# The down projection of a squared-ReLU MLP by seven products of tile sums in chunks 0 to 6

## The chip, the cores and the metric

The kernel runs on one core of one Trainium2 chip. The metric is the device time of one execution in microseconds (us), from runs without a profile; the profile is that of one more execution. TensorE (PE) multiplies, VectorE (DVE) and ScalarE (ACT) work element by element, GpSimd (POOL) and SyncE (SP) issue transfers here, and SBUF and PSUM are the memories on the core: TensorE writes only to PSUM, in banks of 512 floats in each of 128 partitions.

## The reference

One layer of a streaming encoder for 384 tokens: 256 of a new stream and 8 x 16 of running streams. A mixer (a pooling branch and a state-space branch) is followed by the MLP, and the MLP's second product is what the change touches:

```python
D_MODEL = 2048
D_FF = 4 * D_MODEL

x = x + rmsnorm(m, p['g_mix_post'])
hdn = jnp.square(jax.nn.relu(rmsnorm(x, p['g_mlp_pre']) @ p['w_up'])) @ p['w_down']
x = x + rmsnorm(hdn, p['g_mlp_post'])
```

All inputs and outputs are float32.

## The kernel before

**Float32 by three products.** Every operand of a large product is split into a high part, rounded to the format that TensorE multiplies at full speed (`F32R`), and a low part, the rest. A product is then high x high + high x low + low x high, three matmuls into the same bank. `wfetch` (L61) loads a weight tile of 128 x 1024 floats (512 KB) into the ring `w` on SyncE's queue. `wsplit` (L66) makes the high part `wh` on ScalarE (L70) and the low part `wl` on VectorE (L71). The rings `w`, `wh` and `wl` have three tiles each (`wpool`, L39), shared by the up and the down projection.

**Chunks.** The MLP runs in eight chunks (`c8`, L1408) of 1024 hidden channels. The *up stage* of a chunk makes eight hidden tiles (`f8`, L1410): `proj` (L136) multiplies two weight tiles of `w_up` with the 16 tiles of the normed input, 48 matmuls of 384 columns into one bank of `psm` (two banks, L40). VectorE applies the relu and the norm's factor, ScalarE squares, and the result `ht` (channels in the partitions, 384 tokens in the columns) is split into `hh` and `hl`.

The *down stage* multiplies these eight tiles with the chunk's rows of `w_down`, for each of four blocks of 512 output columns (`nb`, L1424): `moving` (L145) takes four weight tiles (`kp`), each with two rows of 128 channels (`k2`), and for each row and each of three blocks `b` of 128 tokens issues the three matmuls of 512 columns (L154 to L156). Here the hidden tile is the stationary operand and the weight moves through. So one `kp` is 18 matmuls and a down stage 4 x 4 x 18 = 288. The three sums of a column block stand in three banks of `pss` (six banks, L41). `done` (L1431) adds each to the accumulator `hacc` in SBUF on VectorE (L1439); in chunk 0 ScalarE copies it there (L1434).

In the last chunk `done` goes on: squares for the norm (L1443), the scale `gpo` (L1445), and behind the last column block the norm's factor, the residual with `x1` (L1455) and the stores of `y`. The very last block's third sum is seeded: ScalarE copies the accumulator into the bank first (L1429) and the matmuls add to it.

**Memory.** `x1` (the residual stream, 3 x 128 x 2048 floats) lies in SBUF from the mixer to the end, as do `gpo`, loaded on GpSimd's queue (L1403) and scaled on ScalarE (L1404), and the split normed input (`x1h`, `x1l`). `mp` and the phase `phf` ahead of the MLP use the right side of SBUF.

**Order.** A tile framework fixes the order of each engine's instructions and all semaphores when the program is made. It does not have to keep the order of the code; where the code wants an order, it says so with `behind`, which the down stage of chunks 0 to 6 does not.

Of the kernel before, what the change touches and what calls it, by code (L numbers as in the profile page):

```python
# [14 lines left out]
P = 128  # L15
T = 384
TP = 256
NB = 8
TS_ = 16
DM = 2048  # L20
# [13 lines left out]
def build(ctx, tc, io):  # L34
    nc = tc.nc
    v, s, te, gp, sy = nc.vector, nc.scalar, nc.tensor, nc.gpsimd, nc.sync

    consts = ctx.enter_context(tc.tile_pool(name="consts", bufs=1))
    wpool = ctx.enter_context(tc.tile_pool(name="wpool", bufs=3))  # L39
    psm = ctx.enter_context(tc.tile_pool(name="psm", bufs=2, space=PSUM))  # L40
    pss = ctx.enter_context(tc.tile_pool(name="pss", bufs=6, space=PSUM))  # L41
    dram = ctx.enter_context(tc.tile_pool(name="dram", bufs=1, space=DRAM))
# [10 lines left out]
    def sstile(name):  # L53
        return pss.tile([P, 512], F32, tag="ss", name=name)
# [51 lines left out]
    bank = [mmtile]  # L106
# [232 lines left out]
    for k in range(4, KD, 2):  # L339
        xsplit(k)  # L340
        xsplit(k + 1)
        hl = esplit(k)
# [780 lines left out]
    r2 = res.tile([P, T], F32, name="r2")  # L1123

    root = [None, None]

# [17 lines left out]
    for b in range(3):  # L1144
        sy.dma_start(x1[:, b, :], io["x_tok"][b])
    NE = 4
    pg0 = ctx.enter_context(tc.tile_pool(name="pg0", bufs=1, reuse_waits="tile"))
    xs2 = []

    def xtiles(pool, n):  # L1150
# [5 lines left out]
    with tc.tile_pool(name="phf", bufs=1, side="right", reuse_waits="tile") as pf, tc.tile_pool(  # L1156
# [119 lines left out]
                {(2, 3): first_turns} if nb == 3 else None,  # L1276
            )
        phk.close()
        pga = ctx.enter_context(tc.tile_pool(name="pga", bufs=1, reuse_waits="tile"))
# [94 lines left out]
        chain[0] = False  # L1374
        for b, i in ((1, 2), (1, 3), (2, 0), (2, 1), (2, 2), (2, 3)):
            square(b, i)
        u20 = chained(io["w_up"][2, 0], "up2_0")
        dgh = pf.tile([P, 3, P], F32R, name="dgh2")
        dgl = pf.tile([P, 3, P], F32R, name="dgl2")
# [13 lines left out]
            last[0] = te.matmul(pairs(bc), onesr, woven(dgl.rearrange("p b t -> p (b t)")), start=False, stop=True)  # L1393
        prod((2,), range(12, KD))
        s.copy(halves(r2), even_odd(bc))
    mpool.close()

    with tc.tile_pool(name="phg", bufs=1, reuse_waits="tile") as pg, tc.tile_pool(
        name="phg2", bufs=2, reuse_waits="tile"
    ) as pg2:  # L1400
        hacc = pg.tile([P, 3, DM], F32, name="hacc")
        gpo = pg.tile([P, DM], F32, name="gpo2")
        gp.dma_start(gpo, io["g_mlp_post"].partition_broadcast(P))  # L1403
        s.activation(gpo, gpo, AF.Copy, scale=-0.5)  # L1404
        st3 = pg.tile([P, 3, 4], F32, name="st3")
        pg.tile([P, 112], F32, name="pad_e")
        NC = 8
        for c8 in range(NC):  # L1408
            hh = []
            for f8 in range(8):  # L1410
                f = c8 * 8 + f8
                ps = ups[f] if f < 3 else proj([io["w_up"][f, 0], io["w_up"][f, 1]], xs2, f"up{f}")
                t = pg2.tile([P, T], F32, tag="t", name=f"ht{f}")
                for c, w in ((slice(0, TP), slice(0, P)), (slice(TP, T), slice(P, 192))):
                    v.scalar_tensor_tensor(
                        out=halves(t[:, c]), in0=even_odd(ps)[:, :, w], scalar=0.0, in1=halves(r2[:, c]), op0=ALU.max, op1=ALU.mult
                    )
                s.activation(t, t, AF.Square)
                h = pg2.tile([P, T], F32R, tag=f"hh{f8}", name=f"hh{f}", bufs=1)
                l = pg2.tile([P, T], F32R, tag=f"hl{f8}", name=f"hl{f}", bufs=1)  # L1420
                s.activation(h, t, AF.Copy)
                v.tensor_tensor(l, t, h.bitcast(F32), ALU.subtract)
                hh.append((h, l))
            for nb in range(4):  # L1424
                o = [sstile(f"wd{c8}_{nb}_{b}") for b in range(3)]
                end = c8 == NC - 1 and nb == 3
                held = 2 if end else None
                if end:
                    s.copy(o[held], hacc[:, held, blk(nb)])  # L1429

                def done(b):  # L1431
                    dst = hacc[:, b, blk(nb)]
                    if c8 == 0:
                        s.copy(dst, o[b])  # L1434
                        return
                    if b == held:
                        dst = o[b]
                    else:
                        v.tensor_tensor(dst, o[b], dst, ALU.add)  # L1439
                    if c8 < NC - 1:  # L1440
                        return
                    q = pg2.tile([P, 512], F32, tag="q3", name=f"q3_{nb}_{b}")
                    s.activation(q, dst, AF.Square, accum_out=st3[:, b, nb : nb + 1])  # L1443
                    if nb < 3:
                        v.tensor_tensor(dst, dst, gpo[:, blk(nb)], ALU.mult)  # L1445
                        return
                    if b == 0:
                        pg.tile([P, 128], F32, name="pad_z")
                    z3 = pg.tile([P, 512], F32, name=f"z3_{b}")
                    v.tensor_tensor(z3, dst, gpo[:, blk(nb)], ALU.mult)  # L1450
                    y = postnorm(pg2, st3, b, "n3", doubled=True)
                    for i in range(4):
                        z = z3 if i == 3 else hacc[:, b, blk(i)]
                        for n, c in enumerate((slice(0, 256), slice(256, 512)) if b + i == 5 else (slice(0, 512),)):
                            v.scalar_tensor_tensor(  # L1455
                                out=z[:, c], in0=z[:, c], scalar=y, in1=x1[:, b, blk(i)][:, c], op0=ALU.mult, op1=ALU.add
                            )
                            (s if n else sy).dma_start(io["y"][b][:, blk(i)][:, c], z[:, c])

                moving(  # L1460
                    o,
                    [(io["w_down"][c8, nb, kp], f"wd{c8}_{nb}_{kp}") for kp in range(4)],
                    hh,
                    4 if end else 0,
                    done,
                    pg,
                    2 if end else 0,
                    held=held,
                )


def _consts(np):
# [121 lines left out]
```

## Time and profile before

| what | us |
|---|---|
| median of 3 runs (2633.67 to 2634.31) | 2634.19 |
| span of the profiled execution (first to last instruction) | 2631.4 |
| up stage of chunk 2 (384 matmuls) | 62.40 |
| down stage of chunk 2 (288 matmuls) | 62.16 |

For the profiled execution the profile gives only the span, not the time around it; median and span are 2.8 us apart. In the profile's rows L is a line of the kernel, the part behind the engine is the operation with its output and inputs by the program's names, then shapes and a count, busy time and mean ns of one, and the idle time of the engine just before them with what ended it. PE is the matmul stream, PEld its weight loads, SPq and POOLq the transfers issued by these engines with their size and the us from issue to landing. In a table of windows each engine has its busy us and its instructions, then follow the granted TensorE clock, the mean busy share of the DMA engines and GB/s.

### The profile page before, as it was taken

Reading aid. Unit: us, or ns where it says so; the run is one execution under the profiler, and the core shown is the slowest. Engines: PE = TensorE matmul, PEld = TensorE weight load, DVE = VectorE, ACT = ScalarE, POOL = GpSimd, SP = SyncE. Lnnn points to the kernel's source line nnn. Section 1 sums busy time; section 2 is a strip of 40 time slices with the busy share of each in tenths; the row PEclk is TensorE's granted clock in tenths of the full one; section 3 lists DMA queues with packets and bytes.
Section 4 is the critical chain, followed back from the end, with each engine's and each line's share of the span. In section 5 each row is a group of like instructions: output and inputs, shape, how many; then the busy total and the mean of one; then the engine's idle time right before and its main releaser. Section 6 shows DMA issues by size and latency. Waiting matters only on the chain.

```text
span 2631.4 us, 40780 instructions
## 1 busy us (share of the span) xinstructions
PE 2621.3 (100%) x16189; PEld 2523.4 (96%) x16189; DVE 1573.0 (60%) x2286; ACT 1159.7 (44%) x1789; POOL 368.6 (14%) x545
## 2 busy tenths in 40 slices
PE   9999999999999999999999999999999999999998
PEld 9999999999999999999999989999999999989897
DVE  6685335799999999967444436434444444444446
ACT  6443324657565756555333336433333333333233
POOL 0000003245444444411000000000000000000000
PEclk9999999999999999999999999999999999999999
DMA  7445446667676767757545544444444444444443
GB/s 276 150 133 156 148 147 223 201 210 238 224 239 211 235 228 238 233 188 260 165 160 160 195 149 133 144 136 136 134 134 135 136 136 136 136 136 136 135 135 131
DMA packets 134256, 456.33 MB, mean 173 GB/s; under 512 B 20545, under 2 KB 27521, under 8 KB 129073
## 3 DMA queue, kind: packets, MB, share of 16 engines
q1 hardware_dynamic: 103552, 361.44, 43.0%
q0 software_dynamic: 23456, 77.47, 8.5%
q10 hardware_dynamic: 7056, 14.81, 1.8%
q8 instruction: 127, 2.08, 0.3%
q14 instruction: 65, 0.52, 0.1%
HBM read 409.27 MB, written 44.37 MB: 172 GB/s over the span
## 4 chain that ended last, share of the span: by engine, by line
PE 99%; DMA 0%; DVE 0%; ACT 0%; SPq 0%; issue 0%; DVEq 0%
PE pj_up L101 6%; PE pj_up L103 6%; PE pj_up L102 6%; PE wd L156 6%; PE wd L155 6%; PE wd L154 6%; PE pj_x L101 5%; PE pj_x L102 5%; PE pj_x L103 5%; PE pj_sp L102 3%; PE pj_z L103 3%; PE pj_z L102 3%; PE pj_z L101 3%; PE pj_sp L103 3%; PE pj_sp L101 3%; PE pj_gb L101 2%
## 5 line engine op out<-in xcount | busy, mean ns | idle before, releaser
L101 PE MATMUL pj_up<-x1h,wh_up 128*128 128x384 f32 (+1 forms) x1024 | 333.7, 326 | 0.0
L103 PE MATMUL pj_up<-x1h,wl_up 128*128 128x384 f32 (+1 forms) x1024 | 333.4, 326 | 0.0
L102 PE MATMUL pj_up<-x1l,wh_up 128*128 128x384 f32 (+1 forms) x1024 | 333.4, 326 | 0.0
L71 DVE TENSOR_TENSOR wl_wd<-w_wd,wh_wd 128x1024 fp32r<-128x1024 f32 x126 | 154.4, 1225 | 240.3 <-ACT wh_wd L70 240.3
L154 PE MATMUL wd<-wh_wd,hh 128*128 128x512 f32 x756 | 286.5, 379 | 0.0
L155 PE MATMUL wd<-wl_wd,hh 128*128 128x512 f32 x756 | 286.5, 379 | 0.0
L156 PE MATMUL wd<-wh_wd,hl 128*128 128x512 f32 x756 | 286.5, 379 | 0.0
L70 ACT ACTIVATE wh_wd<-w_wd 128x1024 fp32r<-128x1024 f32 x126 | 133.1, 1057 | 321.5 <-PE wd L156 261.0
L70 ACT ACTIVATE wh_up<-w_up 128x1024 fp32r<-128x1024 f32 x126 | 133.1, 1057 | 291.9 <-PE pj_up L102 231.7
L71 DVE TENSOR_TENSOR wl_up<-w_up,wh_up 128x1024 fp32r<-128x1024 f32 x126 | 154.4, 1225 | 178.1 <-ACT wh_up L70 178.0
L101 PE MATMUL pj_x<-xgh,wh_x 128*128 128x384 f32 x768 | 251.9, 328 | 0.0
L102 PE MATMUL pj_x<-xgl,wh_x 128*128 128x384 f32 x768 | 250.4, 326 | 0.0
L103 PE MATMUL pj_x<-xgh,wl_x 128*128 128x384 f32 x768 | 250.4, 326 | 0.0
L102 PEld LDWEIGHTS pj_up<-x1l,wh_up 128*128 128x128 f32 x1024 | 193.6, 189 | 0.2
L101 PEld LDWEIGHTS pj_up<-x1h,wh_up 128*128 128x128 f32 x1024 | 193.6, 189 | 0.2
L103 PEld LDWEIGHTS pj_up<-x1h,wl_up 128*128 128x128 f32 x1024 | 193.6, 189 | 0.0
L101 PE MATMUL pj_z<-xgh,wh_z 128*128 128x384 f32 x512 | 166.9, 326 | 0.0
L102 PE MATMUL pj_z<-xgl,wh_z 128*128 128x384 f32 x512 | 166.9, 326 | 0.0
L103 PE MATMUL pj_z<-xgh,wl_z 128*128 128x384 f32 x512 | 166.9, 326 | 0.0
L101 PE MATMUL pj_sp<-abh,wh_sp 128*128 128x384 f32 x512 | 166.9, 326 | 0.0
L102 PE MATMUL pj_sp<-abl,wh_sp 128*128 128x384 f32 x512 | 166.9, 326 | 0.0
L103 PE MATMUL pj_sp<-abh,wl_sp 128*128 128x384 f32 x512 | 166.9, 326 | 0.0
(351 smaller groups left out, 6373.6 us busy)
## 6 DMA issues: line engine op xcount, KB each, us to landing
w_up<-w_up SPq DMA_DIRECT2D x128, 512.0 KB, 3.5
w_wd<-w_down SPq DMA_DIRECT2D x128, 512.0 KB, 3.5
w_x<-w_in SPq DMA_DIRECT2D x96, 512.0 KB, 3.9
w_z<-w_in SPq DMA_DIRECT2D x64, 512.0 KB, 4.4
w_sp<-w_ssd SPq DMA_DIRECT2D x64, 512.0 KB, 3.5
w_ga<-w_ga SPq DMA_DIRECT2D x32, 512.0 KB, 3.6
w_pp<-w_pp SPq DMA_DIRECT2D x32, 512.0 KB, 3.4
hs<-ssm POOLq DMA_DIRECT2D x16, 1024.0 KB, 6.3
```

The lines of the kernel that those rows point to most:

```text
L70: cut[0] = s.activation(h, w, AF.Copy)
L71: cut[1] = v.tensor_tensor(l, w, h.bitcast(F32), ALU.subtract)
L101: te.matmul(out, wh, xh, start=first, stop=False, **how)
L102: te.matmul(out, wh, xl, start=False, stop=False, **how)
L103: return te.matmul(out, wl, xh, start=False, stop=last, **how)
L154: te.matmul(out, mh, vh, start=k == 0 and b != held, stop=False, skip_group_check=b == held)
L155: te.matmul(out, mh, vl, start=False, stop=False, skip_group_check=b == held)
L156: last[0] = te.matmul(out, ml, vh, start=False, stop=k == nk - 1, skip_group_check=b == held)
```

## The change

In chunks 0 to 6 the down stage of two column blocks (a *pair*, `np_`) is computed from sums of tiles. A hidden tile has its ten slots of 128 columns: for channel rows `i` = 1 and 2 (the parity of `kp`), slots 0 to 2 are the three token blocks of row 1 and slots 3 to 5 those of row 2. Slots 6 to 9 and slot 1 are then made on VectorE: s6 = s1 - s4, s7 = s0 - s6, s8 = s3 - s7, s9 = s5 - s2, and s1 becomes s1 - s0. All ten are split in one go (`FH`, `FL`, one pair of tiles for each half `g` of the chunk's channels).

With b11, b12, b21, b22 the weight tiles of channel row i and column block j, the weight sums are U = b11 + b12, V = b12 + b22, W = U + b22 and X = b21 + W. Each of the seven tiles that are used (b11, U, V, b22, W, b21, X) is split and multiplied: for token blocks 0 and 1 seven products m0 to m6 (s0 b11, s3 b21, s8 b22, s4 X, s6 U, s7 W, s1 V), for token block 2 the two sums m7 = s2 b11 + s5 b21 and m8 = s9 b22 + s2 V. These are 11 uses of a weight tile, of 6 matmuls each, for each of two `g`: 132 matmuls for a pair, 264 for a chunk.

U, W and X are added on VectorE, in place. V is made by a transfer on GpSimd's queue that reads b22 once more from HBM and adds it to b12 in SBUF (`accum_op`), behind U's sum. The raw weights lie in nine tiles: two of three in a new ring `wd` of six, the third in `w`.

Each of the nine results has its own accumulator in `acc`. From chunk 1 on m0 to m6 are seeded: ScalarE copies the accumulator into the bank, the matmuls add to it, and ScalarE copies it back; m7 and m8 are added on VectorE as before. m0 to m6 use the six banks of `pss`, m7 and m8 the two of `psm`. In the last chunk's up stage seven sums on VectorE (`converted`) turn the accumulators of the products into those of the output blocks, and the last down stage runs as before, on slots 0 to 5.

For room `x1` is moved to the right side, stored to HBM on GpSimd's queue before the MLP and, with `gpo`, loaded back when the last up product is done and the normed input's room is free. The MLP's tiles now lie on the right side.

```diff
-    x1 = res.tile([P, 3, DM], F32, name="x1")
+    x1 = xp.tile([P, 3, DM], F32, name="x1")
+    x1_scr = [dram.tile([P, DM], F32, name=f"x1_scr{b}") for b in range(3)]
...
+        for b in range(3):
+            gp.dma_start(x1_scr[b], x1[:, b, :])
...
+        HALVES = (("b11", "U", "V"), ("b22", "W", "b21", "X"))
+        USES = {
+            "b11": ((0, 0), (7, 2)),
+            "b21": ((1, 3), (7, 5)),
+            "b22": ((2, 8), (8, 9)),
+            "X": ((3, 4),),
+            "U": ((4, 6),),
+            "W": ((5, 7),),
+            "V": ((6, 1), (8, 2)),
+        }
+        SEEDED = (0, 1, 2, 3, 4, 5, 6)
...
+        def ff_tile(f8, ps, plain):
...
+            s.activation(t, t, AF.Square)
+            if plain:
+                h, l = (a[g][:, p, q * 3 : q * 3 + 3, :].rearrange("p s t -> p (s t)") for a in (FH, FL))
+                s.activation(h, t, AF.Copy)
+                v.tensor_tensor(l, t, h.bitcast(F32), ALU.subtract)
+            elif q:
+                x = V2[p]
+                for o, a, b in ((6, 1, 4), (7, 0, 6), (8, 3, 7), (9, 5, 2), (1, 1, 0)):
+                    v.tensor_tensor(x[:, o], x[:, a], x[:, b], ALU.subtract)
+                s.activation(FH[g][:, p], x, AF.Copy)
+                v.tensor_tensor(FL[g][:, p], x, FH[g][:, p].bitcast(F32), ALU.subtract)
+
+        acc = pg.tile([P, 18, 512], F32, name="acc")
...
+        def raw(name):
+            nraw[0] += 1
+            if nraw[0] % 3 == 0:
+                return wpool.tile([P, 1024], F32, tag="w", name=f"w_{name}")
+            return pg.tile([P, 1024], F32, tag="wd", name=f"w_{name}", bufs=6)
...
+            def form(f, g):
+                k = lambda n: kept[n, g]
+                if f in ("b11", "b21", "b22"):
+                    return load(f, g, int(f[1]), int(f[2]))
+                if f == "U":
+                    kept["b12", g] = load("b12", g, 1, 2)
+                    return add(k("b11"), k("b11"), k("b12"))
+                if f == "V":
+                    gp.dma_start(k("b12"), src(2, 2, g), accum_op=ALU.add)
+                    return k("b12")
+                if f == "W":
+                    return add(k("U"), k("U"), k("b22"))
+                return add(k("b21"), k("b21"), k("W"))
+
+            def taken(m):
+                o, dst = bank[m], acc[:, np_ * 9 + m, :]
+                if c8 == 0 or m in SEEDED:
+                    s.copy(dst, o)
+                else:
+                    v.tensor_tensor(dst, o, dst, ALU.add)
+
+            for part in HALVES:
+                for g in range(2):
+                    for f in part:
+                        w = kept[f, g] = form(f, g)
+                        wh, wl = split(w, f"{f}{c8}_{np_}{g}")
+                        for m, slot in USES[f]:
+                            if m not in bank:
+                                bank[m] = (mmtile if m > 6 else sstile)(f"wd{c8}_{np_}_{m}")
+                                if c8 and m in SEEDED:
+                                    s.copy(bank[m], acc[:, np_ * 9 + m, :])
+                            held = c8 > 0 and m in SEEDED
+                            for k2 in range(2):
...
+                                te.matmul(out, mh, vh, start=begin and not held, stop=False, skip_group_check=held)
+                                te.matmul(out, mh, vl, start=False, stop=False, skip_group_check=held)
+                                te.matmul(out, ml, vh, start=False, stop=end, skip_group_check=held)
+                            if g and final[m] == f:
+                                taken(m)
...
         for c8 in range(NC):
-            hh = []
+            plain = c8 == NC - 1
+            if plain:
+                todo = converted()
             for f8 in range(8):
                 f = c8 * 8 + f8
                 ps = ups[f] if f < 3 else proj([io["w_up"][f, 0], io["w_up"][f, 1]], xs2, f"up{f}")
...
+                ff_tile(f8, ps, plain)
+                if todo:
+                    todo.pop(0)()
+            if not plain:
+                for np_ in range(2):
+                    down_pair(c8, np_)
+        upool.close()
+        pz = ctx.enter_context(tc.tile_pool(name="pz", bufs=1, reuse_waits="tile"))
+        x1 = pz.tile([P, 3, DM], F32, name="x1b")
+        gpo = pz.tile([P, DM], F32, name="gpo2")
+        gp.dma_start(gpo, io["g_mlp_post"].partition_broadcast(P))
+        for b in range(3):
+            gp.dma_start(x1[:, b, :], x1_scr[b])
+        s.activation(gpo, gpo, AF.Copy, scale=-0.5)
```

More of the change, by code (lines that the diff above doesn't have):

```diff
@@ L1146, in build @@
     NE = 4
-    pg0 = ctx.enter_context(tc.tile_pool(name="pg0", bufs=1, reuse_waits="tile"))
+    upool = ExitStack()
+    pg0 = upool.enter_context(tc.tile_pool(name="pg0", bufs=1, reuse_waits="tile"))
     xs2 = []
@@ L1412, in build @@
                 ps = ups[f] if f < 3 else proj([io["w_up"][f, 0], io["w_up"][f, 1]], xs2, f"up{f}")
[L1413 to L1469, printed above, removed]
@@ new lines, in build, with done @@
+        for nb in range(4):
+            o = [sstile(f"wd{c8}_{nb}_{b}") for b in range(3)]
+            end = nb == 3
+            held = 2 if end else None
+            if end:
+                s.copy(o[held], hacc(held, nb))
+            def done(b):
+                dst = hacc(b, nb)
+                if b == held:
+                    dst = o[b]
+                else:
+                    v.tensor_tensor(dst, o[b], dst, ALU.add)
+                q = pz.tile([P, 512], F32, tag="q3", name=f"q3_{nb}_{b}", bufs=2)
+                s.activation(q, dst, AF.Square, accum_out=st3[:, b, nb : nb + 1])
+                if nb < 3:
+                    v.tensor_tensor(dst, dst, gpo[:, blk(nb)], ALU.mult)
+                    return
+                z3 = pz.tile([P, 512], F32, name=f"z3_{b}")
+                v.tensor_tensor(z3, dst, gpo[:, blk(nb)], ALU.mult)
+                y = postnorm(pz, st3, b, "n3", doubled=True)
+                for i in range(4):
+                    z = z3 if i == 3 else hacc(b, i)
+                    for n, c in enumerate((slice(0, 256), slice(256, 512)) if b + i == 5 else (slice(0, 512),)):
+                        v.scalar_tensor_tensor(
+                            out=z[:, c], in0=z[:, c], scalar=y, in1=x1[:, b, blk(i)][:, c], op0=ALU.mult, op1=ALU.add
+                        )
+                        (s if n else sy).dma_start(io["y"][b][:, blk(i)][:, c], z[:, c])
+            moving(
+                o,
+                [(io["w_down"][c8, nb, kp], f"wd{c8}_{nb}_{kp}") for kp in range(4)],
+                hh,
+                4 if end else 0,
+                done,
+                Own,
+                2 if end else 0,
+                held=held,
+            )
```

84 lines of the change are left out of this document (75 added, 9 removed).

## The prediction

> **What bounds the kernel now.** I read the head of the page first, then the chain of work that ended last, then the stage that the change touches.
>
> ```profile
> span 2631.4 us, 40780 instructions
> PE 2621.3 (100%) x16189; PEld 2523.4 (96%) x16189; DVE 1573.0 (60%) x2286; ACT 1159.7 (44%) x1789; POOL 368.6 (14%) x545
> PEclk9999999999999999999999999999999999999999
> PE 99%; DMA 0%; DVE 0%; ACT 0%; SPq 0%; issue 0%; DVEq 0%
> ```
>
> TensorE is never idle, at full clock, and 99% of the chain is its own. So the time is the number of matmuls by the distance between them, and every wait that the change brings to TensorE is paid in full. A matmul's row lasts longer than that distance, because matmuls overlap; the distance I take from starts. These are the first matmul of chunk 2's down stage and the first of the next up stage, in the timeline of PE:
>
> ```profile
> 1938.06 0.38 PE L154 MATMUL wd<-wh_wd,hh 128*128 128x512 f32 x1
> ...
> 2000.22 0.33 PE L101 MATMUL pj_up<-x1h,wh_up 128*128 128x384 f32 x1
> ```
>
> 62.16 us for 4 x 4 x 18 = 288 matmuls is 0.2158 us each. The windows of this down stage and of the up stage behind it show what the others do meanwhile:
>
> ```profile
> 1938.06:2000.22 62.16, 62.16 (x290) 54.44 (x289) 27.75 (x30) 17.85 (x18) 0.00 (x0) 1.00 0.44 135
> 2000.22:2062.62 62.40, 62.40 (x385) 62.40 (x384) 28.12 (x39) 23.50 (x30) 0.00 (x0) 1.00 0.44 135
> ```
>
> In the down stage VectorE is busy 27.8 and ScalarE 17.9 of 62.2 us, GpSimd not at all; DMA is at 0.44.
>
> **What goes: matmuls.** A chunk now has 11 uses of a weight tile where it had 12 (seven for token blocks 0 and 1 instead of eight, four for block 2), so 264 matmuls instead of 288. 24 x 7 chunks x 0.2158 = **36.3 us** less. The last chunk stays as it was.
>
> **What comes, on VectorE and ScalarE.** The durations:
>
> ```profile
> L71 DVE TENSOR_TENSOR wl_wd<-w_wd,wh_wd 128x1024 fp32r<-128x1024 f32 x126 | 154.4, 1225 | 240.3 <-ACT wh_wd L70 240.3
> L850 DVE TENSOR_TENSOR E<-E,cbm 128x1024 f32<-128x1024 f32 x32 | 38.0, 1211 | 0.0
> L1439 DVE TENSOR_TENSOR hacc<-wd,hacc 128x512 f32<-128x512 f32 x83 | 54.9, 691 | 7.9 <-PE wd L156 7.9
> L70 ACT ACTIVATE wh_wd<-w_wd 128x1024 fp32r<-128x1024 f32 x126 | 133.1, 1057 | 321.5 <-PE wd L156 261.0 <-PE pj_up L102 60.4
> L1434 ACT COPY hacc<-wd 128x512 f32<-128x512 f32 x12 | 7.0, 586 | 6.6 <-PE wd L156 6.1
> L1429 ACT COPY wd<-hacc x1: 571/571/571, 2594.7 to 2594.7; 128x512 f32<-128x512 f32 x1
> ```
>
> One pair of column blocks takes TensorE 132 x 0.2158 = 28.5 us. In it VectorE has 14 low parts (1.225), 6 sums of tiles (U, W, X twice; 1.211, by the row of the same shape) and 2 additions for products 7 and 8 (0.691): 17.15 + 7.27 + 1.38 = 25.8 us. ScalarE has 14 high parts, 7 seeds (0.571) and 7 evictions (0.586): 14.80 + 4.00 + 4.10 = 22.9 us. So both fit, but VectorE's share goes from 45% to 90%. It is a little better than that, since VectorE's instructions overlap where neither waits:
>
> ```profile
> 1997.63 1.23 DVE L71 TENSOR_TENSOR wl_up<-w_up,wh_up 128x1024 fp32r<-128x1024 f32 x1 [2.66 <-ACT wh_up L70]
> 1999.13 1.99 DVE L1439 TENSOR_TENSOR hacc<-wd,hacc 128x512 f32<-128x512 f32 x3 [0.28 <-PE wd L156]
> ...
> 2009.15 1.22 DVE L71 TENSOR_TENSOR wl_up<-w_up,wh_up 128x1024 fp32r<-128x1024 f32 x1 [0.31 <-ACT wh_up L70]
> 2010.29 0.55 DVE L1422 TENSOR_TENSOR hl<-ht,hh 128x384 fp32r<-128x384 f32 x1
> ```
>
> The last two start 1.14 us apart, 0.08 less than the first lasts; with that on 22 instructions the pair is 24.0 us. The load is uneven. The second half of a pair (b22, W, b21, X twice) has 8 low parts, 4 sums and 2 additions, 16.0 us by durations and 14.9 by distances, against 72 matmuls, 15.5 us; the first half only 6 and 2, 9.8 us against 13.0. The rings wh and wl hold three tiles, so little of the first half's slack carries over. The term lies between nothing and the 0.5 us by which 16.0 exceeds 15.5 plus as much again for hand-overs between the two engines; I take 0.25 per pair, 14 pairs: **+4 us**.
>
> The first two rows answer what stands behind a wait: the low part of the next stage's weight stands ahead of the accumulator's addition, which the code has earlier. So the order on an engine is not the code's, and an eviction or seed that waits for TensorE or a bank need not hold up the next split. Seven banks of a pair go through the six of pss; each seed has a bank that was evicted two tiles or more earlier, so I cost seeds and evictions nothing beyond their time above; without that cover a seed ahead of its product costs 0.57 us, up to 98 x 0.57 = 56 us, part of the rivals below.
>
> **The accumulating transfer.** V is b12 + b22, added by a transfer from GpSimd's queue that waits for U's sum on VectorE (which reads b12). Behind it on that queue stands only the next V, and at the end the loads of gpo and x1. V's split waits for it on ScalarE, and TensorE for that. How long may it take? b11 cannot be split before TensorE has left the tile three before; from there to V it issues two tiles (3 uses in either place), b11 (2) and U (1): 36 matmuls, 7.8 us. Off that go b11's parts 1.06 + 1.23, the sum 1.21 and V's high part 1.06; 3.2 us are left. No accumulating transfer is in the trace; the nearest rows:
>
> ```profile
> w_wd<-w_down SPq DMA_DIRECT2D x128, 512.0 KB, 3.5
> hs<-ssm POOLq DMA_DIRECT2D x16, 1024.0 KB, 6.3
> ...
> mar<-ma_scr POOLq DMA_DIRECT2D x16, 192.0 KB, 3.8
> gbr<-gb_scr POOLq DMA_DIRECT2D x16, 192.0 KB, 2.6
> ...
> gpo<-g_mlp_post POOLq DMA_DIRECT2D x1, 1024.0 KB, 4.9
> ...
> L683 POOL DMA_DIRECT2D hs<-ssm x16 | 9.0, 560 | 8.7 <-DMA new_ssm_s<-hs 7.4 <-PE pj_z L102 1.3
> ```
>
> From below it is a plain 512 KB load, 3.5 us; from above, as it must read its destination too, a 1 MB load on GpSimd's queue, 6.3; GpSimd's own 0.56 comes on top. Between 192 KB (mean 3.2) and 1 MB (mean 5.6), 512 KB is 4.1; I take 5, being nearer to the loads of that queue with something for the second read, so 5.6 with the issue. Then V is late by 2.4 us if nothing takes its place (0.9 to 3.7 by the two ends). What can take it: b11 of the other half, 12 matmuls, 2.6 us, if the order puts it ahead. As the order follows readiness by the rows above, I take it that most is covered: 0.4 us late each, 28 transfers: **+11 us** (ends: 0 and 28 x 3.7 = 104).
>
> [...]
>
> **From up to down.** The first half's second K part (g = 1) needs the last up tiles in their ten-slot form.
>
> ```profile
> L1422 DVE TENSOR_TENSOR hl<-ht,hh 128x384 fp32r<-128x384 f32 x64 | 35.3, 552 | 0.6 <-ACT hh L1421 0.6
> L1421 ACT ACTIVATE hh<-ht 128x384 fp32r<-128x384 f32 x64 | 33.8, 529 | 2.0
> L1418 ACT ACTIVATE ht<-ht 128x384 f32<-128x384 f32 x64 | 32.4, 507 | 0.7 <-DVE ht L1415 0.7
> 2008.22 0.62 DVE L1415 SCALAR_TENSOR_TENSOR ht<-pj_up,r 128x256 f32<-128x256 f32 x2 [1.75 <-PE pj_up L103]
> ```
>
> From 384 to 1024 columns VectorE's subtraction grows by 1.05 ns per column and ScalarE's copy by 0.83, so 128 columns are 0.28, 1280 columns 1.49 and 1.27 us (estimates). The chain behind the last up matmul: 0.62 + 0.51 + 5 x 0.28 + 1.27 + 1.49 = 5.3 us. Its cover is g = 0 of b11, U and V, 30 matmuls, 6.5 us. But the low parts of V and of the next b11 fall into the same time on VectorE, 2.45 us: 7.7, at worst 1.3 late. I take 0.6 for 7 chunks: **+4 us**. In the up stage itself the ten-slot form adds 4 x (5 x 0.28 + 1.49) - 8 x 0.55 = 7.2 us to VectorE's 28.1 of 62.4, and in the last chunk the seven conversion sums 7 x 1.21 = 8.5: hidden by the matmuls.
>
> **The rest, at nothing.** x1 goes out on GpSimd's queue, and comes back with gpo once the last up product has freed the room.
>
> ```profile
> new_ssm_s<-hs POOLq DMA_DIRECT2D x16, 1024.0 KB, 4.3
> 1630.78 0.54 POOL L1403 DMA_DIRECT2D gpo<-g_mlp_post  x1 [162.97 <-DVE x L1178]
> 1648.71 1.15 DVE L1415 SCALAR_TENSOR_TENSOR ht<-pj_up,r 128x256 f32<-128x256 f32 x4 [0.57 <-ACT r L1395]
> ...
> 2560.70 0.33 PE L103 MATMUL pj_up<-x1h,wl_up 128*128 128x384 f32 x1
> L1445 DVE TENSOR_TENSOR hacc<-hacc,gpo x9: 682/684/686, 2577.2 to 2611.1; 128x512 f32<-128x512 f32 x9
> L1455 DVE SCALAR_TENSOR_TENSOR hacc<-hacc,n_n,x x9: 744/747/752, 2615.4 to 2626.7; 128x512 f32<-128x512 f32 x9
> ```
>
> x1 is final at 1630.8 and three stores of 4.3 end at 1643.7, before the first hidden tile is written at 1648.7 into what may be its room; uncovered, 5 us once. From 2560.7 there are 16 us for gpo (4.9 and a scaling) and 55 for 4 MB (4 x 6.3 = 25). Loads per pair grow from 8 to 10 of 512 KB: 5.2 MB in 28.5 us, 184 GB/s, against the 135 above, through nine raw tiles instead of three.
>
> **Sum.** -36.3 + 4 + 11 + 4 = -17 on a span of 2631.4: 2614. The median of the three runs, 2634.2, is 2.8 above the span; with that **2617 us**.
>
> **Rivals.**
> 1. *All of it is hidden.* V in time, 0.25 per pair and 0.6 per chunk or less: 36 less 8 to 0, so 2598 to 2606; I put it at 2605. For it: 3.2 us of cover and 2.6 more if b11 goes ahead, and idle time on GpSimd. Against: 90% on VectorE.
> 2. *VectorE becomes the bound.* Second halves run at 16.0 us plus two hand-overs that stay open, about 1 us: 1.5 x 14 = 21, with V's 11 and the 4 at the change of stage 36: **2634**, no change. For it: ScalarE's waits for VectorE and back at each tile (240 us in the row of L71). Against: the measured distances, 14.9 in 15.5.
> 3. *V is late, and nothing else is ready: slower.* The place is TensorE's wait for V's high part, twice a pair. With 8 us for the other terms it decides from (36.3 - 8) / 28 = 1.0 us late. With 6.2, midway between the 5.6 taken and the upper end of 6.9, against a cover of 3.2 that the other b11 stretches by half of its 2.6 us on the mean, 1.7 is left; 28 x 1.7 = 48: 2634 - 36 + 8 + 48 = **2654**. For it: the upper row; the fixed order, since a transfer longer than the order reckons with cannot be made up. Against: the lower rows. [...]
>
> **Chances.** Forecast (2610 to 2628) 0.40, all hidden 0.22, VectorE's bound 0.13, V late 0.25. The range, 2600 to 2653, leaves out the lowest quarter of the second case (0.06) and of the last what lies beyond a lateness of 1.7 us (half of it, 0.12). A measurement of this kernel can tell 0.2%, 5 us: faster 0.62, same 0.13, slower 0.25.
>
> **What would show it.** Right: 264 matmuls in a chunk's down stage at 0.216; PE's idle time under 3 us per chunk, most of it ahead of V's tiles and at the first g = 1 tile; V's landing near 5. Wrong: a landing above 7, or below 4; PE's waits at W and X, released by VectorE (rival 2); an order in which V stands ahead of the next b11 in every pair (rival 3). The forecast falls most easily with the 0.4 us per V, since each 0.1 us is 2.8 us.

## The result and the profile after

| | before | after |
|---|---|---|
| median, us | 2633.93 (same chip) | **2741.23** (4 runs, 2739.8 to 2742.94) |
| span of the profiled execution, us | 2631.4 | 2738.0 |
| down stage of chunk 2, us | 62.16 | 77.55 |
| up stage of chunk 3, us | 62.40 | 62.40 |

The ratio is 1.0409, 95% interval 1.0396 to 1.0421: 4.1% slower. The forecast was 2617, with 2653 as the upper end: the direction and the range were both wrong. The head of the page of after:

```profile
span 2738.0 us, 41060 instructions
PE 2640.3 (96%) x16021; PEld 2508.0 (92%) x16021; DVE 1788.9 (65%) x2525; ACT 1337.5 (49%) x2019; POOL 396.3 (14%) x579
```

The matmuls that were to go are gone: 16189 - 16021 = 168 = 24 x 7. But TensorE, which was busy for 100% of the span, is now busy for 96%. The windows show where; chunk 2's down stage and the up stage behind it (us, busy us of PE, PEld, DVE, ACT, POOL with their instructions, then the granted clock, the DMA share and GB/s):

```profile
1967.54:2045.09 77.55, 64.64 (x267) 52.09 (x266) 50.51 (x50) 42.95 (x55) 2.59 (x3) 0.93 0.48 129
2045.09:2107.49 62.40, 62.40 (x386) 62.40 (x385) 34.33 (x52) 25.40 (x30) 0.87 (x1) 1.00 0.47 145
```

264 matmuls at 0.2158 us would take 57.0 us; the stage takes 77.55. Two things are lost in it: PE is not busy for 12.9 us, and the clock in it is 0.93, not 1.00. The up stage is as before, and so is the end: the last down stage began 70.7 us ahead of the span's end, 70.6 before. All seven changed down stages are alike (76.6 to 78.1), so the loss of 20 us each is the whole story. The waits of PE in that part of the trace (us in total, times, longest):

```profile
PE wd L1521 <- ACT wh_V L1466: 63.3, 23, 3.5
PE wd L1522 <- DVE wl_U L1467: 10.2, 14, 0.8
PE wd L1522 <- DVE wl_V L1467: 9.4, 14, 0.8
PE wd L1521 <- ACT wh_U L1466: 3.0, 6, 0.5
PE wd L1523 <- DVE fl L1450: 1.1, 6, 0.2
```

TensorE waits for V's high part at 23 of its 28 places, and ScalarE, which makes that part, waits for the transfer (the waits of the whole trace):

```profile
ACT wh_V L1466 <- DMA w_b<-w_down: 102.2, 26, 5.2
```

One of these places, chunk 2, first pair, second half of the channels, in the timeline of all engines (start us, us, engine, line, operation, output and inputs; in brackets the idle time ahead of it and what ended it):

```profile
1976.44 1.22 DVE L1480 TENSOR_TENSOR w_b<-w_b,w_b 128x1024 f32<-128x1024 f32 x1
...
1978.19 0.86 POOL L1491 DMA_DIRECT2D w_b<-w_down  x1 [12.50 <-DVE w_b L1480]
...
1981.09 0.38 PE L1523 MATMUL wd<-wh_U,fl 128*128 128x512 f32 x1
...
1983.85 1.06 ACT L1466 ACTIVATE wh_V<-w_b 128x1024 fp32r<-128x1024 f32 x1 [3.94 <-DMA w_b<-w_down]
...
1984.95 1.22 PE L1521 MATMUL wd<-wh_V,fh 128*128 128x512 f32 x2 [3.48 <-ACT wh_V L1466]
...
1986.80 0.63 PE L1523 MATMUL wd<-wh_V,fl 128*128 128x512 f32 x1
...
1987.22 0.63 PE L1521 MATMUL wd<-wh_V,fh 128*128 128x512 f32 x1
```

U's sum ends at 1977.66; GpSimd begins to issue V's transfer 0.53 us later; ScalarE has V at 1983.85, 6.2 us behind the sum. TensorE has done U's last matmul at 1981.47 and has nothing in its order but V. Behind the wait the matmuls start 0.42 us apart, twice the usual distance. Two windows, behind this wait of 3.48 us and behind a shorter one of 2.28 us in the next pair, show that this is the clock:

```profile
1984.95:1990.60 5.65, 5.61 (x12) 4.02 (x13) 3.57 (x3) 3.99 (x6) 0.00 (x0) 0.50 0.44 152
...
2026.02:2030.40 4.38, 3.82 (x16) 3.05 (x17) 3.57 (x3) 4.35 (x7) 0.00 (x0) 1.00 0.37 124
```

0.50 behind the long wait, 1.00 behind the short one. So this wait of 3.5 us cost more than itself. V's matmuls carry the mark in their mean durations (groups by line; busy us, mean ns, idle time ahead):

```profile
L1522 PE MATMUL wd<-wl_V,fh 128*128 128x512 f32 x112 | 55.3, 494 | 9.6 <-DVE wl_V L1467 9.4
L1521 PE MATMUL wd<-wh_V,fh 128*128 128x512 f32 x112 | 55.0, 527 | 63.4 <-ACT wh_V L1466 63.3
L1523 PE MATMUL wd<-wh_V,fl 128*128 128x512 f32 x112 | 52.4, 468 | 0.0
```

468 to 527 ns for V, where a matmul at full clock lasts 0.38 us (U's last in the timeline above). To count the loss I took, for every matmul of the PE timeline, what its start lies beyond the usual distance from the start before it (0.2158 us for 512 columns). That gives 142.7 us: 87.2 are idle time that a wait ended (63.3 of it for V's high part), 42.8 are larger distances without a wait, and 12.7 lie beside the waits. The timeline's rows are rounded, so these parts are good to about half a microsecond. Less the 36.3 us of matmuls saved, 142.7 gives +106.4; the two spans differ by 106.6.

### The profile page after: what moved, and what is told of

Same layout as the page of the kernel before. It is cut to its first block, busy times and chain, and to the rows that moved or that the text cites. A ratio compares the mean times of both kernels' runs of the same rounds, so it can differ in the third digit from the quotient of the medians.

```text
span 2738.0 us, 41060 instructions
## 1 busy us (share of the span) xinstructions
PE 2640.3 (96%) x16021; PEld 2508.0 (92%) x16021; DVE 1788.9 (65%) x2525; ACT 1337.5 (49%) x2019; POOL 396.3 (14%) x579
## 3 DMA queue, kind: packets, MB, share of 16 engines
q8 instruction: 126, 2.06, 0.3%
## 5 line engine op out<-in xcount | busy, mean ns | idle before, releaser
L1491 POOL DMA_DIRECT2D w_b<-w_down x28 | 24.2, 865 | 924.6 <-ACT fh L1449 477.8
L71 DVE TENSOR_TENSOR wl_sp<-w_sp,wh_sp 128x1024 fp32r<-128x1024 f32 x64 | 78.3, 1224 | 116.6 <-ACT wh_sp L70 116.6
L70 ACT ACTIVATE wh_sp<-w_sp 128x1024 fp32r<-128x1024 f32 x64 | 67.8, 1060 | 166.2 <-PE pj_sp L102 158.2
L101 PEld LDWEIGHTS pj_x<-xgh,wh_x 128*128 128x128 f32 x768 | 145.1, 189 | 2.1 <-issue 0.4
L103 PEld LDWEIGHTS pj_x<-xgh,wl_x 128*128 128x128 f32 x768 | 145.1, 189 | 0.5 <-DVE wl_x L71 0.5
```

The lines of the kernel that those rows point to most:

```text
L70: cut[0] = s.activation(h, w, AF.Copy)
L71: cut[1] = v.tensor_tensor(l, w, h.bitcast(F32), ALU.subtract)
L101: te.matmul(out, wh, xh, start=first, stop=False, **how)
L103: return te.matmul(out, wl, xh, start=False, stop=last, **how)
L1491: gp.dma_start(k("b12"), src(2, 2, g), accum_op=ALU.add)
```

## The experiments

The first four undo or move one thing about V. Theory A in them is that V's accumulating transfer is late at a fixed place; it is rival 3 of the prediction with a larger price.

**1. No transfer.** V is b12 as it was loaded for U: b22 is left out of V.

```diff
                 if f == "V":
-                    gp.dma_start(k("b12"), src(2, 2, g), accum_op=ALU.add)
                     return k("b12")
```

> Leaves out the addition of b22 to V: V is b12 as loaded, no transfer on GpSimd's queue; all else is as after the change. Theory A (TensorE waits for the accumulating transfer, 63 us in 23 waits of up to 3.5 us, and then runs on a halved clock for some microseconds): both go, down stages near 59 to 62 us instead of 77.3, time 2615 to 2635. Theory B (the hand-overs between a VectorE and a ScalarE at 80 to 90% load cost TensorE its time, and V's split is only where they show): the time stays within 10 us of 2741.

2625.96 us, ratio to before 0.997 (0.9959 to 0.9981). Theory A's time; theory B falls. The transfer is worth 115 us of the 2741, and without it the change is faster than before. The chunk's window and all of PE's waits:

```profile
1937.42:1998.47 61.05, 58.56 (x266) 49.46 (x266) 49.80 (x50) 42.50 (x55) 0.00 (x0) 1.00 0.40 130
```

```profile
PE wd L1521 <- DVE wl_U L1467: 8.9, 15, 0.7
PE wd L1521 <- DVE wl_V L1467: 5.6, 14, 0.4
PE wd L1520 <- ACT wh_V L1466: 2.8, 6, 0.5
```

The clock is 1.00 again. The stage is 4.1 us above 57.0, though, and by the same count 28.3 us are still lost in the kernel: hand-overs at U and V, which are there without any transfer.

**2. V behind both U.** The transfer stays; only the order of the weight tiles is moved, so that V comes into the pair's second half.

```diff
-        HALVES = (("b11", "U", "V"), ("b22", "W", "b21", "X"))
+        HALVES = (("b11", "U"), ("V", "b22", "W", "b21", "X"))
```

> Only the order of the weight tiles changes: both U first, V at the head of the second part, so that b11 and U of the other half (18 matmuls, 3.9 us) stand between U's sum and V. Theory A: the transfer has 3.9 us more and the waits of 3.5 us go, with them the slow clock; down stages 58 to 63 us, time 2610 to 2640. Theory B: the same work in another order, 2720 to 2760.

2629.28 us, 0.9981 (0.9971 to 0.999). The two longest waits of PE:

```profile
PE wd L1521 <- ACT wh_U L1466: 7.9, 7, 1.2
PE wd L1521 <- ACT wh_V L1466: 3.2, 7, 0.5
```

V's high part is waited for 3.2 us in all, not 63.3, with the same transfers on the same queue (landing 5.5 us here too): what cost the time is the place of V in the order, not the transfer as such. U's high part is waited for 7.9 us, 3.0 in after; the first half now has two tiles to work on where it had three.

**3. V on VectorE.** b22 is loaded at V's place and added there, as U is. The tile is kept for b22's own products, so b22 is read from HBM once and not twice.

```diff
-                if f in ("b11", "b21", "b22"):
+                if f == "b22":
+                    return k("b22")
+                if f in ("b11", "b21"):
...
                 if f == "V":
-                    gp.dma_start(k("b12"), src(2, 2, g), accum_op=ALU.add)
-                    return k("b12")
+                    kept["b22", g] = load("b22", g, 2, 2)
+                    return add(k("b12"), k("b12"), k("b22"))
```

> V is added on VectorE from a b22 that is loaded earlier, with no accumulating transfer; VectorE gets 2 more sums of 1.21 us per pair. Theory A: 1.2 us in the place of 6.2, the long waits go; VectorE's load of 26 to 28 us per pair now lies at TensorE's 28.5, so some waits of about 1 us stay: 2625 to 2665. Theory B: VectorE's load is the cause, so it gets slower, above 2745.

2632.96 us, 0.9997 (0.9988 to 1.0007): the change's loss is gone, and its gain too. 28 more sums are 28 x 1.21 = 34 us of VectorE's time, and the kernel is 7 us above experiment 1. So most of VectorE's added work is hidden, which speaks against VectorE as the bound.

**4. A tile of its own for V.** b12 is loaded twice, and the transfer adds to the second copy, so that it need not wait for U's sum.

```diff
                     kept["b12", g] = load("b12", g, 1, 2)
+                    kept["own", g] = load("own", g, 1, 2)
                     return add(k("b11"), k("b11"), k("b12"))
                 if f == "V":
-                    gp.dma_start(k("b12"), src(2, 2, g), accum_op=ALU.add)
-                    return k("b12")
+                    gp.dma_start(k("own"), src(2, 2, g), accum_op=ALU.add)
+                    return k("own")
```

> b12 is loaded a second time into a tile of its own, and the transfer adds b22 there without waiting for U's sum; order and VectorE's work as after the change, two loads of 512 KB more per pair. Theory A: the transfer can start tiles ahead, the long waits and the slow clock go: 2610 to 2640, if the raw ring leaves room. Theory B: 2735 to 2750.

2626.42 us, 0.9972 (0.9962 to 0.9982), within 0.5 us of experiment 1, with the transfer in place and nothing left out. It lands even later, counted from its issue:

```profile
w_own<-w_down POOLq DMA_DIRECT2D x28, 512.0 KB, 7.5
```

7.5 us instead of 5.5, and TensorE does not notice, since the transfer no longer waits for U's sum. What mattered is the chain of U's sum, the issue and the landing behind it, which starts too late for V's place.

**5. Sums not in place.** Experiment 4, and U is written over the first b12 and X over W, so that a sum need not wait until the tile that it overwrote has been split.

```diff
-                    return add(k("b11"), k("b11"), k("b12"))
+                    return add(k("b12"), k("b11"), k("b12"))
...
-                return add(k("b21"), k("b21"), k("W"))
+                return add(k("W"), k("b21"), k("W"))
```

> As the run with a second b12, and U is written over the first b12 and X over W, so that neither sum waits for the split of b11 or b21. The run with a second b12 still loses 4 us per down stage, at the low parts of U and V. Theory C (the chain split of b11, sum U, split of U costs it): down stages 57.5 to 59.5 us, time 2605 to 2618. Theory D (VectorE's load, whatever the order of its sums): within 3 us of 2626.

2622.94 us, 0.9959 (0.9946 to 0.9973): 3.5 us better than experiment 4, and far less than was hoped. The waits at U and V are gone, and two of seven chunks reach the ideal, as this one:

```profile
2060.30:2117.32 57.02, 57.02 (x266) 49.81 (x265) 49.11 (x49) 44.06 (x56) 3.45 (x4) 1.00 0.73 206
```

The others take 58.4 to 63.2, and there TensorE waits for low parts of b and X:

```profile
PE wd L1523 <- DVE wl_b L1467: 9.3, 7, 2.8
PE wd L1523 <- DVE wl_X L1467: 4.7, 6, 0.8
```

In this run the sums on VectorE wait 20.2 us for loads (14 times); in experiment 4 none did. Experiment 11 shows one such place.

**6. The transfer without its addition.** V's tile is a plain load of b22 on GpSimd's queue, into a tile of its own: b12 is left out of V.

```diff
+                    kept["own", g] = raw(f"own{c8}_{np_}{g}")
...
-                    gp.dma_start(k("b12"), src(2, 2, g), accum_op=ALU.add)
-                    return k("b12")
+                    gp.dma_start(k("own"), src(2, 2, g))
+                    return k("own")
```

> V's tile is loaded by a plain transfer of 512 KB on GpSimd's queue instead of an accumulating one; leaves out b12 in V. It measures the price: if adding is what makes the accumulating transfer take 5.5 us to land, the plain one lands in 3.5 to 4.2; if it is GpSimd's queue, in 5 or more. GpSimd's own time per issue, 0.86 us, falls to 0.56 in the first case. Time as with the second b12, 2620 to 2630.

2626.08 us in a single run, as experiments 1 and 4. Its use is the price of the addition. After, issue on GpSimd and landing:

```profile
L1491 POOL DMA_DIRECT2D w_b<-w_down x28 | 24.2, 865 | 924.6 <-ACT fh L1449 477.8
...
w_b<-w_down POOLq DMA_DIRECT2D x28, 512.0 KB, 5.5
```

This experiment, the group of the issues and the row of the landing:

```profile
L1492 POOL DMA_DIRECT2D w_own<-w_down x28 | 14.8, 529 | 804.9 <-DVE wl_b L1467 360.9 <-DVE w_b L1480 191.3 <-DVE wl_up L71 134.7
```

```profile
w_own<-w_down POOLq DMA_DIRECT2D x28, 512.0 KB, 3.7
```

The transfer that adds takes 1.8 us more to land (5.5 against 3.7) and 0.33 us more to issue (0.86 against 0.53). The plain one also goes into another tile and need not wait for U's sum; what that does to its landing was not tried alone.

**7. No seeds.** Experiment 5 with every result added by VectorE, none seeded by ScalarE.

```diff
-        SEEDED = (0, 1, 2, 3, 4, 5, 6)
+        SEEDED = ()
```

> As the run whose sums are not in place, but no product is seeded: VectorE adds all nine to their accumulators, 7 x 0.69 us more per pair, 30.6 us by durations and 28.3 by distances against TensorE's 28.5; ScalarE is relieved of 14 copies. If VectorE's load can bound the stage, this shows its price: 2 us or more per pair, 2635 to 2660. If distances and idle gaps suffice, within 5 us of the run with seeds.

2620.26 us, 0.9954 (0.9939 to 0.9968): not slower than experiment 5, by three runs from 2619.94 to 2624.85. By the prediction's durations VectorE now has 14 x 1.225 + 6 x 1.211 + 9 x 0.691 = 30.6 us of work in a pair whose matmuls take 28.5, and the kernel keeps its pace on the whole. VectorE's instructions overlap: by the distance that the prediction read from the rows, 0.08 us less for each of 29, it is 28.3 us. Rival 2, in which VectorE's load sets the pace, is refuted.

**8. The gap filled.** After, with twelve more matmuls into a bank that nobody reads, between U and V: 28 x 12 x 0.2158 = 72.5 us of added work.

```diff
-                                te.matmul(out, ml, vh, start=False, stop=end, skip_group_check=held)
+                                last[0] = te.matmul(out, ml, vh, start=False, stop=end, skip_group_check=held)
...
+                        if f == "U":
+                            fill = sstile(f"fill{c8}_{np_}{g}")
+                            with behind(last[0]):
+                                for _ in range(12):
+                                    te.matmul(fill, ..., start=True, stop=True)
```

> The changed kernel with 12 extra matmuls of 512 columns into a spare bank of PSUM, behind the last matmul of each product with U and ahead of V's: 28 times 12 is 336, by 0.2158 us each 72.5 us of work that the result doesn't need. They stand where TensorE now waits for V. Theory F (part of the lost time is the clock, which falls by half behind a wait of 3.1 us or more): the 2.6 us that the twelve take leave waits of 0.5 to 0.9 us of the 3.1 to 3.5, none above 3, and the matmuls behind them run 0.22 us apart from the first on; about 63 us of waiting and about 45 us of slow matmuls go, 72.5 come: 2700 to 2725, below the changed kernel in spite of the added work. Theory G (only the wait is lost, and the slow matmuls have another cause, such as V's tiles themselves or VectorE and the transfer beside them): the distances of 0.43 us stay, the waiting alone is replaced by work, and where no wait was (one place of four in a chunk) 2.6 us are added: 2741 to 2765.

2741.35 us: as after, with 72.5 us more work. Theory F's time was missed, and the measured one lies at the lower edge of G's; but G falls by the rows it named. V's matmuls (groups by line) and the waits of PE:

```profile
L1521 PE MATMUL wd<-wh_V,fh 128*128 128x512 f32 x112 | 45.7, 408 | 16.0 <-ACT wd L1513 8.5 <-ACT wh_V L1466 7.3
L1522 PE MATMUL wd<-wl_V,fh 128*128 128x512 f32 x112 | 45.2, 404 | 14.9 <-DVE wl_V L1467 14.9
L1523 PE MATMUL wd<-wh_V,fl 128*128 128x512 f32 x112 | 43.1, 385 | 0.0
```

```profile
PE wd L1522 <- DVE wl_V L1467: 14.9, 20, 0.8
PE wd L1521 <- ACT wd L1513: 8.5, 6, 2.2
PE wd L1522 <- DVE wl_X L1467: 8.5, 12, 0.8
PE wd L1521 <- ACT wh_V L1466: 7.3, 14, 0.7
```

The same V tiles, the same transfers, and the means fall from 468 to 527 ns to 385 to 408: the slow matmuls belonged to the waits. By the count of distances, 42.8 us of larger distances are now 10.4. The idle time fell by 40.4 us only (87.2 to 46.8) and not by 63, since V's low part, X's and the seeds (L1513) are late in turn, and 3.2 more lie beside the waits: 72.5 - 32.4 - 40.4 + 3.2 = 2.9 us, and the spans differ by 3.4 (2741.4 to 2738.0).

**9 and 10. Seeds for one half of the pair only.** Experiment 5 with other lists of seeds, first those of the second half's products, then those of the first half's.

```diff
-        SEEDED = (0, 1, 2, 3, 4, 5, 6)
+        SEEDED = (1, 2, 3, 5)
```

> The kernel of e5 with seeds only for the products of tile sums of the second half (1, 2, 3 and 5), so that the first half's three (0, 4, 6) are added by VectorE, which has fewer sums of weights to form in that half. Theory: the waits that are left in e5 (about 4 us in four of seven chunks) come from ScalarE being late with its share of casts and seeds; with three seeds fewer in a chunk its queue is shorter, and the time is 2612 to 2620. Rival: they come from the loads of b and the order of the sums, seeds change nothing: 2620 to 2626.

```diff
-        SEEDED = (0, 1, 2, 3, 4, 5, 6)
+        SEEDED = (0, 4, 6)
```

> The kernel of e5 with seeds only for the first half's products (0, 4 and 6), so that the second half's four are added by VectorE in the same stretch in which it forms the weight sums. If VectorE's load in the second half decides (theory: it becomes the bound there), waits for U, X or the low parts appear there and the time is 2625 to 2640. If it doesn't, the time stays with e5 and the kernel without seeds: 2618 to 2626.

2618.03 us, 0.994 (0.9925 to 0.9955), and 2616.14, 0.9933 (0.9916 to 0.9949). Number 9 lies in its theory's range, but its reason cannot be the whole one, as 10 takes away the other four seeds and 7 all of them, and 10 is the fastest of the three. Neither theory of 10 gave its time: it lies 2 us below the lower of the two ranges. VectorE's load in the second half, which should have made it slow, does not. How long the sums on VectorE wait for loads doesn't explain the times either: it is 20.2 us in experiment 5, 14.6 in 9, 11.2 in 7 and 11.1 in 10, but the profiled executions took 2620.80, 2617.54, 2624.85 and 2615.40, so that 7 waits as little as 10 and is the slowest of the four. Why the seeds move the time stays open. **Number 10 is the best version found: 0.7% faster than before**, and PE is busy for 99% of the span:

```profile
span 2613.6 us, 41056 instructions
PE 2594.1 (99%) x16021; PEld 2491.0 (95%) x16021; DVE 1808.5 (69%) x2573; ACT 1288.7 (49%) x1923; POOL 395.1 (15%) x579
```

**11 and 12. Both cures, or the cheaper one.** Number 11 is experiment 10 with the order of experiment 2; number 12 has that order, X over W and the seeds of 10, but no second load of b12.

```diff
-        HALVES = (("b11", "U", "V"), ("b22", "W", "b21", "X"))
+        HALVES = (("b11", "U"), ("V", "b22", "W", "b21", "X"))
```

> The kernel of e10 (own second load of b12, U and X over the loads that are done with, seeds for the first half's products 0, 4 and 6 only) with V moved behind both U, as in e2. Theory: e2's order takes the cover of V from 3.2 us to more than the transfer needs, and e10's tiles free the buffers earlier; together fewer waits are left than the 18 us of loss in e10: 2600 to 2614. Rival: with V in the second half VectorE and ScalarE, which there form W, X and their parts, have two weights more to split in the same stretch, and the first half runs short for its two blocks (e2 waited 7.9 us there for U's high part): 2614 to 2628.

> Order of e2 (V behind both U), X written over W, seeds for 0, 4 and 6 only, and no second load of b12: U in b11's place, the transfer into b12 as in the changed kernel. It has the smallest edit: two lines of order and tiles and the list of seeds. If the second load of b12 and its buffers are not needed once V stands later (theory), the time is within 4 us of e11; if the transfer's wait for U still holds V up, or a buffer comes free later without them, it is 5 to 15 us above e11, near e2's 2629.

2627.29 us, 0.9975 (0.9964 to 0.9987), and 2623.48, 0.9959 (0.9944 to 0.9974). Two cures are worse than one, by 11 us against experiment 10. The rival's time holds, but not by the wait that it named: U's high part is not waited for, and nearly all of the waiting is for low parts of b (16.7 us, 11 times). VectorE's timeline of number 11:

```profile
2208.81 2.36 DVE L1480 TENSOR_TENSOR w_b<-w_b,w_b 128x1024 f32<-128x1024 f32 x2 [3.54 <-DMA w_b<-w_down]
2211.09 0.68 DVE L1503 TENSOR_TENSOR acc<-wd,acc 128x512 f32<-128x512 f32 x1
2211.69 1.21 DVE L1467 TENSOR_TENSOR wl_b<-w_b,wh_b 128x1024 fp32r<-128x1024 f32 x1
```

and PE's:

```profile
2212.96 0.48 PE L1523 MATMUL wd<-wl_b,fh 128*128 128x512 f32 x1 [3.35 <-DVE wl_b L1467]
2213.28 0.38 PE L1524 MATMUL wd<-wh_b,fl 128*128 128x512 f32 x1
2213.49 0.38 PE L1522 MATMUL wd<-wh_b,fh 128*128 128x512 f32 x1
```

A sum waits 3.54 us for a load; the low part of b, three instructions behind it on VectorE, waits with it, and TensorE waits 3.35 us for that low part. It is V's case again in another place: a transfer that is later than the fixed order has room for, with needed work behind the waiter. Why the loads are late there was not tried. Number 12 does without it (no sum waits for a load there), and is within 4 us of 11, on the faster side, as its theory had it: once V stands later, the second load of b12 isn't needed.

## Why the prediction was wrong

**What bounds the kernel: right.** Every wait of TensorE was paid in full, and more than that.

**Matmuls, -36.3: right.** 168 fewer, at 0.216 us: 57.02 us for 264 in experiment 5.

**The accumulating transfer, +11: this step failed.** Its parts were near the mark. A landing of 5 us was taken and 5.5 measured; from U's sum to V 5.6 were taken and 6.2 measured; uncovered, V was to be late by 2.4 us (0.9 to 3.7), and the wait shown above is 3.48. The mean over all 28 places is 63.3 / 28 = 2.3. What failed is the sentence "As the order follows readiness by the rows above, I take it that most is covered: 0.4 us late each". The rows showed that the order is not the code's. They did not show that it knows a transfer's true length. In after V stands directly behind U at TensorE, and the next b behind V. Experiment 2 makes by hand an order like the one that I took for granted, and the waits go. By the count of distances after loses 142.7 us and experiment 1 28.3: the transfer costs 114.4, of which 60.5 are V's wait (63.3 less the 2.8 that are left without transfer), 38.0 larger distances (42.8 less 4.8) and 15.9 shorter waits and what lies beside them.

**The clock: no term.** About a quarter of the loss, 38.0 of 142.7 us, is larger distances that come with the transfer: matmuls at half speed behind waits, for which the prediction had no term in any of its cases. Experiment 8 takes 32.4 of these us away by filling the wait with work.

**VectorE's tightness and the change of stage, +4 each: too small together, 28 for 8.** Experiment 1 has nothing but these, and loses 28.3 us. The new tiles' low part is waited for only 1.1 us in after and not at all in experiment 1, so the change of stage is near nothing. The rest are hand-overs at U and V, 0.7 us at the most each. VectorE's load alone doesn't make them (experiment 7, with more of it, has none at U and V). Part of them is an order again: when U's sum no longer overwrites b11, it can go ahead of b11's low part, and the waits for U's and V's parts are gone (experiment 5), though waits for low parts of b and X, with late loads ahead of them, then take most of the gain back.

**The rest, at nothing: right.** The last stage took 70.7 us after 70.6, the up stages 62.40. In the aside on uncovered seeds the count was off: chunk 0 has none, so they are 84 and not 98; no term rests on it.

In all: -36.3 + 28.3 + 114.4 = +106.4, where -17 was forecast.

**Rival 3 was the case**, with its mechanism and its sign, and its point of decision at 1.0 us. Its 2654 is short by 87: 66.4 from V (114.4 where it had 48: a mean wait of 2.3 us and not 1.7, the clock, and what lies beside the waits) and 20.3 from the hand-overs (28.3 for 8). The upper end of the range was taken from it, so the range failed with its price: a rival that had lateness as a cost per us had no place for a wait that also slows what comes behind it.

**Rival 1**, all hidden, 2605, was reached by none of these versions. Experiment 10 comes out at 2616.14, beside the forecast of 2617, but that is another kernel, with loads, tiles and seeds that the prediction didn't count; it doesn't bear the sum out. **Rival 2** is refuted by experiment 7; that the changed kernel without its transfer, 2625.96, lies between the forecast and this rival's 2634 comes from the hand-overs.

## What to carry to other kernels

Where an order is fixed when the program is made, ask of every new transfer not what could cover it but what stands behind it in that order; if its length isn't known from a trace, put its consumer further back by hand, or free its start of what it waits for. Where matmuls are dense, price long waits at more than their length: here the clock added about half (32.4 us on 60.5). The next section shows which waits these were here. And expect the next late transfer in the same place: a cure that adds loads can make another one late.

## What the runs showed of the hardware

**In after the clock fell behind waits.** All 14 waits for V of 3.1 to 3.5 us were followed by 0.43 us between matmuls, where 0.2158 is usual, for 4 to 12 of them, at a granted clock of 0.50; of the six of 2.2 to 2.6 us none was. It need not be one long wait. After, chunk 4:

```profile
2252.40 0.48 PE L1521 MATMUL wd<-wh_V,fh 128*128 128x512 f32 x1 [1.10 <-ACT wh_V L1466]
2253.66 0.48 PE L1522 MATMUL wd<-wl_V,fh 128*128 128x512 f32 x1 [0.78 <-DVE wl_V L1467]
...
2254.24 0.63 PE L1521 MATMUL wd<-wh_V,fh 128*128 128x512 f32 x1
2254.67 0.63 PE L1522 MATMUL wd<-wl_V,fh 128*128 128x512 f32 x1
```

Waits of 1.10 and 0.78 us with one matmul between them were followed by the half rate as well. In this trace the granted clock fell 15 times ahead of the kernel's end, each time to 0.50 and for 3.41 or 6.83 us, one or two steps of 3.41 us; and these stretches begin a whole number of such steps apart, wherever the waits lie: the first three at 1704.59, 1735.31 (9 steps later) and 1844.53 (32 more). In the step just ahead of each of the 15 PE was idle for 1.88 to 3.36 us. Two steps of after, behind the first a step of 0.50 and behind the second none:

```profile
1701.18:1704.59 3.41, 1.35 (x5) 0.86 (x5) 1.88 (x2) 0.00 (x0) 0.00 (x0) 1.00 1.00 150
1704.59:1711.42 6.83, 4.85 (x11) 3.40 (x12) 3.59 (x3) 4.02 (x5) 0.00 (x0) 0.50 0.35 87
...
2022.03:2025.44 3.41, 1.71 (x8) 1.15 (x7) 0.62 (x1) 1.11 (x2) 0.00 (x0) 1.00 0.66 125
```

In the first PE is idle for 2.06 us, in the last for 1.70. Two more steps, with 1.67 and 1.84 us, were not followed by a fall either. A wait that lay in two steps could cost nothing more than itself: the 2.62 us that ended at 1746.58 have 1.59 us in one step and 1.03 in the next, the clock stayed at 1.00, and soon behind them the matmuls started 0.22 us apart. The 3.35 us of experiment 11, shown above, were followed by 0.32 and 0.21. So the length of a wait alone did not decide it. All figures of the steps are from one trace, and no limit for other kernels follows from them.

**The transfer that added took longer.** In after 512 KB landed 5.5 us after the issue, which took 0.86 us; the plain transfer of experiment 6 took 3.7 and 0.53, so 1.8 and 0.33 us less. In experiment 4, beside more loads, the adding one landed after 7.5 us; why was not tried.
